# The first 512 tokens' attention output stored as two float16 halves and turned by transposing DMAs, and the sums of squares spread by one bfloat16 product

## The chip, the cores and the metric

The kernel runs on one core of one Trainium2 chip. Its engines are named here as the profile names them: PE (TensorE, matrix products), PEld (its loading of weights), DVE (VectorE), ACT (ScalarE), POOL (GpSimd) and SP (SyncE, which here does nothing but issue DMAs). Each engine runs its own instructions strictly in order, and an instruction that waits holds back all that stand behind it on that engine. The metric is the device time of one execution in microseconds (us), less being better.

## The reference

One decoder layer over 2048 tokens of width 1024, in which two mixers share a normalised input and one output projection:

```python
h = rms_norm(x, g_pre[l]) * (1.0 + scale[:, None, :]) + shift[:, None, :]
proj = h @ w_in[l]
qa, ka, va, fa, za, qb, kb, vb, zb = jnp.split(proj, split_points, axis=-1)
oa = forgetting_attention(qa, ka, va, fa + b_fgate[l])     # 8 heads of 64, causal
oa = oa * jax.nn.silu(za)
qb, kb = rope(qb, positions), rope(kb, positions)
ob = sliding_window_sink_attention(qb, kb, vb, sinks[l])   # window of 128, 8 query heads
ob = ob * jax.nn.silu(zb)
y = jnp.concatenate([oa, ob], axis=-1) @ w_out[l]
x = x + gate[:, None, :] * rms_norm(y, g_post[l])
```

(The reshapes into heads are left out.) What matters for the change is the piece between the two attentions and the last product: the attention output `o` of 2048 x 1024, with tokens as rows, is multiplied elementwise by the gates `z` and then enters the product with `w_out`. For that product the features must lie on the partitions, so `o` has to be turned (transposed) on its way.

## The kernel before

**Stages.** The 2048 tokens are 16 tiles of P = 128, or 4 chunks of CH = 512, numbered `ci`; the 1024 features are KT = 8 slices of 128. The stages follow one another: normalisation, the input projection with the window attention beside it, the forgetting attention of heads 0 to 7 (20 steps to a head, two key blocks of 128 to a step: two steps for chunk 0, then four, six and eight), and the output projection of tiles 0 to 15, whose first pieces are mixed into the steps of head 7. Large products are made of float16 halves: a float32 value is written as `hi + lo`, with `hi` its float16 rounding and `lo` the rest, and three float16 products take the place of one in float32.

**Order of the work.** The program is one hand-made list. A counter `tick()` advances twice in each attention step, and `after(n, f)` puts `f` into the list n ticks later. Each engine executes its instructions in the order in which that list issues them; waits come from data and from buffers in use.

**Attention step.** On PE the scores (L1349, L1350, on the diagonal L1352) write one buffer `sta`; ACT takes the exponential (L1356, `p`) and its float16 half (L1360, `pha`); DVE takes the rest by a subtraction (L1363); two steps later PE multiplies by the values (L1373, L1375, L1376). There is one `sta`, so the scores of the next step wait for L1356. At a chunk's last step DVE normalises the sum into `ona` (L1380, L1382).

**Storing the attention output.** `o_store` (L283) takes a result of 512 tokens (64 features of a head) to memory. For chunks 1 to 3 ACT makes the float16 half (L295, after `lag` ticks), one tick later DVE makes the rest (L291), and one DMA stores both (L292) into `o_d[ci]`, which holds the two halves of each tile. For chunk 0 one DMA stores the float32 values at once (L285). The window attention issues these DMAs on POOL, the forgetting attention on SP. The gates `z` are written to memory earlier, already turned (`z_d`).

**Turning it.** `Out.load` (L1464) brings one tile's `o` and gates into pieces of two buffers `T`, all of it issued by SP: for tiles 0 to 3 a plain load of the 128 x 1024 float32 rows (L1479), for tiles 4 to 15 two transposing DMAs (L1483), one for each half; then the gates (L1485). `Out.turn(lag)` (L1487) follows some ticks later. For tiles 0 to 3 it begins with eight PE transposes (L1492) into two PSUM banks `px`. Then, each in a tick of its own: `gate` on DVE, which for tiles 0 to 3 multiplies the two banks by the gates (L1502) and for the others first adds the halves (L1505) and then multiplies (L1506); `squares_` on ACT (L1510), which sums the squares along each partition into `gs`; `scale_`, where PE multiplies `gs` by a matrix of ones (L1514) so that each partition receives the total, and DVE makes a power of two of it (L128, L129, L1518, L1519); then the scaled halves for the product, on ACT (L1524) and on DVE (L1525). The product itself is L1576 on PE.

**When.** The loads of tiles 0 and 1 are issued at steps 4 and 6 of head 7, their turns at steps 6 and 8; those of tiles 2 and 3 come with the first pieces of the output projection, all inside head 7, which ends at about 1000 us. Around them SP also loads the output weights (L1433), which ACT and DVE split into halves `wohl` (L1442, L1443), and two rows of row maxima for the scores (L1263). L392 and L396 belong to the gates of the last heads, L351 to their projection.

Of the kernel before, what the change touches and what calls it, by code (L numbers as in the profile page):

```python
# [10 lines left out]
F32 = mybir.dt.float32  # L11
F16 = mybir.dt.float16
BF16 = mybir.dt.bfloat16
# [3 lines left out]
ALU = mybir.AluOpType  # L17
AX = mybir.AxisListType

P = 128  # L20
S = 2048
D = 1024
KT = D // P
NB = S // P
CH = 512
NCH = S // CH
# [17 lines left out]
def hybrid_layer(  # L44
# [17 lines left out]
    V, A, G, PE, SP = nc.vector, nc.scalar, nc.gpsimd, nc.tensor, nc.sync  # L62
# [6 lines left out]
    dram = ctx.enter_context(tc.tile_pool(name="dram", bufs=1, space=DRAM))  # L69
# [5 lines left out]
    const = ctx.enter_context(tc.tile_pool(name="const", bufs=1))  # L75
    small = ctx.enter_context(tc.tile_pool(name="small", bufs=4))

    o_d = [dram.tile([CH, D], F32, name="o_d0")] + [dram.tile([4, 2, P, D], F16, name=f"o_d{t}") for t in range(1, NCH)]
    z_d = dram.tile([KT, P, S], F32, name="z_d")
    mx_d = [dram.tile([P, 1], F32, name=f"mx_d{n}") for n in range(3)]  # L80

# [1 line left out]
    def sm(n, tag):  # L83
        return small.tile([P, n], F32, tag=tag, name=tag)
# [71 lines left out]
    ident = const.tile([P, P], F32, name="ident")  # L156
# [8 lines left out]
    ones = const.tile([P, P], F32, name="ones")  # L165
# [36 lines left out]
    def after(n, f):  # L202
        late.append([n, f])
# [77 lines left out]
        w_low(key, 0, 1)  # L281

    def o_store(on, pool, ci, rows_, cols_, eng, lag):  # L283
        if ci == 0:
            eng.dma_start(o_d[0][rows_, cols_].rearrange("(u p) c -> p u c", p=P), on)  # L285
            return
        u0, u1 = rows_.start // P, rows_.stop // P
        oh = pool.tile([P, u1 - u0, 2, on.shape[-1]], F16, tag="oh", name="oh")

        def low():  # L290
            V.tensor_tensor(oh[:, :, 1], on, oh[:, :, 0], op=ALU.subtract)  # L291
            eng.dma_start(o_d[ci][u0:u1, :, :, cols_].rearrange("u n p c -> p (u n) c"),  # L292
                          oh[:].rearrange("p u n c -> p (u n) c"))

        after(lag, lambda: A.activation(oh[:, :, 0], on, AF.Copy))  # L295
        after(lag + 1, low)
# [166 lines left out]
    start = ExitStack()  # L463
# [998 lines left out]
    class Out:  # L1462
# [5 lines left out]
        def load(self):  # L1468
            t = self.t
            rows_ = slice(t * P, (t + 1) * P)  # L1470
            n = t % 2 if t < 4 or t % 4 > 1 else 2 + t % 2
            T, n = Ts[n // 2], n % 2
            if T is Ts[0]:
                o, z = T[:, n, :], T[:, 2 + n, :]
            else:
                o, z = T[:, 2 * n, :], T[:, 2 * n + 1, :]
            if t < 4:
                self.o = o.bitcast(F32)
                SP.dma_start(self.o, o_d[0][rows_, :])  # L1479
            else:  # L1480
                self.oT = o.rearrange("p (l k n) -> p l k n", l=2, k=KT)
                for n in range(2):
                    SP.dma_start_transpose(self.oT[:, n], o_d[t // 4][t % 4, n])  # L1483
            self.z = z.bitcast(F32).rearrange("p (k n) -> p k n", k=KT)
            SP.dma_start(self.z, z_d[:, :, rows_].rearrange("k p n -> p k n"))  # L1485

        def turn(self, lag):  # L1487

            if self.t < 4:
                px = [bk[bank()][:].rearrange("p (k n) -> p k n", k=4) for _ in range(2)]  # L1490
                for k in range(KT):
                    PE.transpose(px[k // 4][:, k % 4, :], self.o[:, k * P:(k + 1) * P], ident[:])  # L1492
            self.hl = wpool.tile([P, 2, KT, P], F16, tag=("whl", "wraw")[self.t % 2], name="oz")
            self.sc = sm(1, "w_pw")
            hi, lo = self.hl[:, 0], self.hl[:, 1]
            gs = sm(1, "w_mx")

            def gate():
                if self.t < 4:
                    for h in range(2):  # L1500
                        z = self.z[:, 4 * h:4 * h + 4, :]
                        V.tensor_tensor(z, px[h], z, op=ALU.mult)  # L1502
                    return
                of = ozp.tile([P, KT, P], F32, tag="of", name="of")
                V.tensor_tensor(of[:], self.oT[:, 0], self.oT[:, 1], op=ALU.add)  # L1505
                V.tensor_tensor(self.z, of[:], self.z, op=ALU.mult)  # L1506

            def squares_():
                junk = stp.tile([P, KT, P], BF16, tag="st", name="zj")
                A.activation(junk[:], self.z, AF.Square, accum_out=gs[:])  # L1510

            def scale_():
                pg = bk[bank()][:, 0:1]
                PE.matmul(pg, ones[:], gs[:], start=True, stop=True)  # L1514
                root_scale(self.sc[:], pg)

                self.inv = sm(1, "w_sw")
                V.tensor_tensor(self.inv[:], self.sc[:], ysc[:], op=ALU.mult)  # L1518
                V.reciprocal(self.inv[:], self.inv[:])  # L1519

            after(1, gate)
            after(2, squares_)
            after(lag, scale_)
            after(lag + 1, lambda: A.activation(hi, self.z, AF.Copy, scale=self.sc[:]))  # L1524
            after(lag + 2, lambda: V.scalar_tensor_tensor(lo, self.z, self.sc[:], hi, op0=ALU.mult, op1=ALU.subtract))  # L1525
# [258 lines left out]
```

## Time and profile before

| | us |
|---|---|
| three executions | 1157.04, 1157.98, 1157.98 |
| their median | 1157.98 |
| the profiled execution | 1157.8 |
| its span, first to last instruction | 1156.1 |
| PE busy | 1116.8 (97%) |
| DVE busy | 930.5 (80%) |
| ACT busy | 661.4 (57%) |
| POOL busy | 207.5 (18%) |
| DMA, the whole span | 120.10 MB, mean 104 GB/s |

The profiled execution's time lies 1.7 us above its span: this is what passes around the first and the last instruction. A row of the time line gives the start in us, the duration in us, the engine (with q behind it: its sequencer, which issues and waits), the line of the kernel, the operation, `output<-input`, the shape, and in square brackets how long the engine stood idle just before and which engine, tile and line released it. `x8` in such a row means that eight instructions of a kind in a row are shown as one. Buffer numbers are left out, so `bk` is any PSUM bank and `T` any of the two big buffers. A row of the windows gives for a stretch of time the busy time of each engine with its number of instructions, the granted clock of PE, the busy share of the DMA engines, and what they moved.

### The profile page before, as it was taken

To read this page: it belongs to the slowest core of one execution; us is meant where nothing else is said; L and a number is where in the kernel's file an instruction comes from. 1 tells how busy PE (TensorE), PEld (TensorE's weight loads), DVE (VectorE), ACT (ScalarE), POOL (GpSimd) and SP (SyncE) were. 2 spreads that over 40 slices of the span, in tenths; PEclk is the share of its full clock that TensorE was granted. 3 is DMA by queue.
4 is the path that set the end of the run, shared out by engine and by line. 5 is a ranking of instruction groups with operands and counts; after the bars stand their busy time and mean duration, and the time that the engine had idled before them with its cause. 6 is when DMAs were issued, how large, how long until landed. Compare 5 with 4: busy or idle time off the path is not lost. (4 is left out here: it accounts for less than half of the span.)

```text
span 1156.1 us, 25291 instructions
## 1 busy us (share of the span) xinstructions
PE 1116.8 (97%) x9869; PEld 656.3 (57%) x9869; DVE 930.5 (80%) x2137; ACT 661.4 (57%) x1150; POOL 207.5 (18%) x332
## 2 busy tenths in 40 slices
PE   5899999999999999999999999999999999999997
PEld 2475544577765866555555555555555555544444
DVE  7877468987888568788988899888888887878885
ACT  2876344654555421666757666666776778534332
POOL 1122134554556530010010110001000000000000
PEclk9899999999999999999999999999999999999999
DMA  9943355433243232442344342123311337686743
GB/s 333 336 116 72 87 78 96 97 63 90 52 92 88 58 87 58 73 108 29 80 64 87 84 67 70 38 49 76 45 43 34 91 101 206 140 225 197 199 135 109
DMA packets 123476, 120.10 MB, mean 104 GB/s; under 512 B 64948, under 2 KB 100828, under 8 KB 123356
## 3 DMA queue, kind: packets, MB, share of 16 engines
q1 hardware_dynamic: 112088, 85.69, 27.6%
q0 software_dynamic: 10832, 32.50, 13.5%
q8 instruction: 77, 1.26, 0.6%
q14 instruction: 43, 0.35, 0.1%
q10 hardware_dynamic: 436, 0.28, 0.1%
HBM read 64.75 MB, written 25.18 MB: 78 GB/s over the span
## 5 line engine op out<-in xcount | busy, mean ns | idle before, releaser
L1356 ACT ACTIVATE p<-sta,lift,scl_qk 128x1024 f32<-128x1024 f32 (+2 forms) x160 | 172.0, 1075 | 131.6 <-PE sta L1350 82.6
L351 PE MATMUL bk<-hT,wh_qk 128*128 128x512 f16 x768 | 194.7, 378 | 0.0
L1363 DVE TENSOR_TENSOR pha<-p,pha 128x1024 f16<-128x1024 f32 (+2 forms) x160 | 169.1, 1057 | 0.2 <-ACT pha L1360 0.2
L1303 DVE TENSOR_REDUCE a_m<-bk 128x1 f32<-128x512 f32 x192 | 130.4, 686 | 45.8 <-PE bk L1300 44.8
L1576 PE MATMUL bk<-wohl,oz 128*128 128x512 f16 x744 | 165.3, 379 | 1.1 <-DVE oz L1525 0.7
L1360 ACT ACTIVATE pha<-p 128x1024 f16<-128x1024 f32 (+2 forms) x160 | 148.1, 926 | 5.9 <-PE poa L1376 1.2
L1576 PEld LDWEIGHTS <-oz 128*128 128x128 f16 x744 | 71.9, 99 | 82.8 <-DVE oz L1525 1.8
L1376 PE MATMUL poa<-vt,pha 128*128 128x65 f16 x1088 | 116.1, 192 | 1.4 <-DVE pha L1363 1.2
L1373 PE MATMUL poa<-vt,pha 128*128 128x65 f16 x1088 | 116.6, 193 | 0.8 <-DVE ona L1382 0.7
L1375 PE MATMUL poa<-vt,pha 128*128 128x64 f16 x1088 | 116.6, 194 | 0.0
L351 PEld LDWEIGHTS <-wh_qk 128*128 128x128 f16 x768 | 72.1, 97 | 74.4 <-issue 2.1
L1349 PE MATMUL sta<-T 128*128 128x512 f16 (+1 forms) x320 | 110.9, 346 | 2.8 <-ACT p L1356 2.7
L1300 PE MATMUL bk<-T 66*128 66x512 f16 (+2 forms) x320 | 109.7, 348 | 2.4 <-DVE a_m L1303 1.9
L1373 PEld LDWEIGHTS <-pha 128*128 128x128 f16 x1088 | 101.5, 96 | 15.5 <-DVE ona L1382 1.9
L1350 PE MATMUL sta<-T 69*128 69x512 f16 (+1 forms) x320 | 109.8, 348 | 0.0
L1375 PEld LDWEIGHTS <-pha 128*128 128x128 f16 x1088 | 100.9, 97 | 11.4
L1376 PEld LDWEIGHTS <-pha 128*128 128x128 f16 x1088 | 100.8, 99 | 1.8 <-DVE pha L1363 1.7
L351 PE MATMUL bk<-hT,wh_za 128*128 128x512 f16 x384 | 99.7, 378 | 0.0
L369 PE MATMUL bk<-wh_va,hT 128*128 128x256 f16 x768 | 91.9, 273 | 0.0
L351 PE MATMUL bk<-hT,wh_zb 128*128 128x512 f16 x384 | 91.6, 379 | 0.2 <-DVE qc L754 0.2
L351 PE MATMUL bk<-hT,wh_qb 128*128 128x512 f16 x384 | 91.2, 379 | 0.0
L369 PEld LDWEIGHTS <-hT 128*128 128x128 f16 x768 | 73.3, 98 | 12.2 <-issue 2.1
(459 smaller groups left out, 1919.7 us busy)
## 6 DMA issues: line engine op xcount, KB each, us to landing
hT<-in_x_dram SPq DMA_DIRECT2D x20, 512.0 KB
wa<-in_w_ada_dram SPq DMA_DIRECT2D x16, 512.0 KB
z_d<-tz POOLq DMA_DIRECT2D x32, 256.0 KB, 3.0
T<-z_d SPq DMA_DIRECT2D x16, 512.0 KB
T<-stq SPq DMA_DIRECT2D x62, 128.0 KB
out_dram<-hT SPq DMA_DIRECT2D x15, 512.0 KB
xt<-in_x_dram SPq DMA_DIRECT2D x12, 512.0 KB
qs<-qf SPq DMA_DIRECT2D x80, 64.0 KB
```

The lines of the kernel that those rows point to most:

```text
L351: PE.matmul(ps, whl[:, a, k, :], hT[ci][:, b, k, :], start=(k == 0 and n == 0), stop=(k == KT - 1 and n == 2))
L369: PE.matmul(ps[:, (u % 2) * 2 * P:(u % 2 + 1) * 2 * P], hT[ci][:, a, k, u * P:(u + 1) * P], wv[p][:, b, k, :], start=(k == 0 and n == 0), ...
L1303: V.tensor_reduce(m3[:, u, pc:pc + 1], mx[:, :w], axis=AX.X, op=ALU.max)
L1349: PE.matmul(self.st[:, o:o + w], T[:, 3, kb_], T[:, 1, qc], start=True, stop=False)
L1350: PE.matmul(self.st[:, o:o + w], T[0:XR, 2, kb_], T[0:XR, 0, qc], start=False, stop=not diag)
L1356: A.activation(self.p32[:, :self.w], self.st[:, :self.w], AF.Exp, scale=scl[f"qk{self.hd}"][:], bias=lift[:])
L1360: A.activation(self.ph[:, 0, :self.w], self.p32[:, :self.w], AF.Copy)
L1363: V.tensor_tensor(self.ph[:, 1, :self.w], self.p32[:, :self.w], self.ph[:, 0, :self.w], op=ALU.subtract)
L1373: PE.matmul(po[:, u, :], ph[:, 0, pq], vt[:, b, hd, 0:65], start=(self.first and n == 0 and u == 0), stop=False)
L1375: PE.matmul(po[:, u, 0:64], ph[:, 0, pq], vt[:, b, hd, 65:VW], start=False, stop=False)
L1376: PE.matmul(po[:, u, :], ph[:, 1, pq], vt[:, b, hd, 0:65], start=False, stop=(self.last and n == len(self.blocks) - 1))
L1576: PE.matmul(py, self.hl[:, i, k, :], w_slot(8 * j + k)[:, cc], start=(k == 0 and m_ == 0), stop=(k == KT - 1 and m_ == 2))
```

## The change

`o_d[0]` gets the form that the other chunks have, so the special case for chunk 0 in `o_store` is gone: the eight float32 stores of the window attention and the eight of the forgetting attention become a copy on ACT, a subtraction on DVE and a store of the two halves. Each of tiles 0 to 3 is loaded by two transposing DMAs in place of one plain load, and its eight PE transposes are gone. Its `gate` now adds the two halves into a PSUM bank and multiplies that bank by the gates, bank by bank, which is four DVE operations of 128 x 512 where there were two. For all 16 tiles the product that spreads `gs` over the partitions takes the upper 16 bits of its float32 operands as bfloat16, which drops the lower bits of the sums; the result sets only a power of two, by which a tile is scaled for its float16 halves and which is divided out again.

```diff
-    o_d = [dram.tile([CH, D], F32, name="o_d0")] + [dram.tile([4, 2, P, D], F16, name=f"o_d{t}") for t in range(1, NCH)]
+    o_d = [dram.tile([4, 2, P, D], F16, name=f"o_d{t}") for t in range(NCH)]
...
     def o_store(on, pool, ci, rows_, cols_, eng, lag):
-        if ci == 0:
-            eng.dma_start(o_d[0][rows_, cols_].rearrange("(u p) c -> p u c", p=P), on)
-            return
         u0, u1 = rows_.start // P, rows_.stop // P
...
-            if t < 4:
-                self.o = o.bitcast(F32)
-                SP.dma_start(self.o, o_d[0][rows_, :])
-            else:
-                self.oT = o.rearrange("p (l k n) -> p l k n", l=2, k=KT)
-                for n in range(2):
-                    SP.dma_start_transpose(self.oT[:, n], o_d[t // 4][t % 4, n])
+            self.oT = o.rearrange("p (l k n) -> p l k n", l=2, k=KT)
+            for n in range(2):
+                SP.dma_start_transpose(self.oT[:, n], o_d[t // 4][t % 4, n])
...
                 px = [bk[bank()][:].rearrange("p (k n) -> p k n", k=4) for _ in range(2)]
-                for k in range(KT):
-                    PE.transpose(px[k // 4][:, k % 4, :], self.o[:, k * P:(k + 1) * P], ident[:])
...
             gs = sm(1, "w_mx")
+            gs1 = gs[:].bitcast(BF16)[:, 1:2]
...
                     for h in range(2):
-                        z = self.z[:, 4 * h:4 * h + 4, :]
-                        V.tensor_tensor(z, px[h], z, op=ALU.mult)
+                        hs = slice(4 * h, 4 * h + 4)
+                        V.tensor_tensor(px[h], self.oT[:, 0, hs], self.oT[:, 1, hs], op=ALU.add)
+                        V.tensor_tensor(self.z[:, hs], px[h], self.z[:, hs], op=ALU.mult)
                     return
...
-                PE.matmul(pg, ones[:], gs[:], start=True, stop=True)
+                PE.matmul(pg, ones[:].bitcast(BF16).rearrange("p (n two) -> p two n", two=2)[:, 1], gs1, start=True, stop=True)
```

Lines behind `o_store` have numbers that are three smaller after the change, and those behind the removed transposes differ by more.

The order of the instructions shows two places. The first is SP in head 7, from the last stores of chunk 0 and 3 to the loads of tiles 0 and 1 (`o_d_69` is chunk 0's, `sv` and `hT_110` take output weights). Before:

```order
L292 DMA o_d_72<-oh 128x8x64
L1433 DMA sv<-in_w_out_dram 128x512
L285 DMA o_d_69<-ona 128x4x64
L1479 DMA T_6055<-o_d_69 128x1024
L1485 DMA T_6055<-z_d 128x8x128
L1263 DMA T_6056<-rw 2x4x128
L1433 DMA hT_110<-in_w_out_dram 128x512
L1479 DMA T_6055<-o_d_69 128x1024
L1485 DMA T_6055<-z_d 128x8x128
```

With the change:

```order
L289 DMA o_d_72<-oh 128x8x64
L1430 DMA sv<-in_w_out_dram 128x512
L289 DMA o_d_69<-oh 128x8x64
L1476 DMA_TRANSPOSE T_6079<-o_d_69 128x8x128 x2
L1478 DMA T_6079<-z_d 128x8x128
L1260 DMA T_6080<-rw 2x4x128
L1430 DMA hT_110<-in_w_out_dram 128x512
L1476 DMA_TRANSPOSE T_6079<-o_d_69 128x8x128 x2
L1478 DMA T_6079<-z_d 128x8x128
```

No DMA has changed its place; the store now takes its data from `oh`, which DVE writes two ticks after `ona`, and two transposing DMAs stand where the plain loads stood.

The second place is DVE in the same stretch, from the step behind chunk 0's last result to the gate of tile 0. Before:

```order
L1320 TENSOR_SCALAR lq_1696<-a_mr 128x4
L1363 TENSOR_TENSOR pha<-p_13661,pha 128x1024
L392 TENSOR_SCALAR tz<-tz,bk_6030 128x512
L1363 TENSOR_TENSOR pha<-p_13707,pha 128x896
L1443 TENSOR_SCALAR wohl<-sv,wsc,wohl 128x512
L1363 TENSOR_TENSOR pha<-p_13755,pha 128x384
L1443 TENSOR_SCALAR wohl<-sv,wsc,wohl 128x512
L1502 TENSOR_TENSOR T_6055<-bk_138,T_6055 128x512
L1502 TENSOR_TENSOR T_6055<-bk_136,T_6055 128x512
L1363 TENSOR_TENSOR pha<-p_13801,pha 128x1024
```

With the change:

```order
L1360 TENSOR_TENSOR pha<-p_13706,pha 128x1024
L288 TENSOR_TENSOR oh<-ona,oh 128x4x64
L389 TENSOR_SCALAR tz<-tz,bk_6054 128x512
L1360 TENSOR_TENSOR pha<-p_13752,pha 128x896
L1440 TENSOR_SCALAR wohl<-sv,wsc,wohl 128x512
L1360 TENSOR_TENSOR pha<-p_13804,pha 128x384
L1440 TENSOR_SCALAR wohl<-sv,wsc,wohl 128x512
L1494 TENSOR_TENSOR bk_138<-T_6079 128x512
L1495 TENSOR_TENSOR T_6079<-bk_138,T_6079 128x512
L1494 TENSOR_TENSOR bk_136<-T_6079 128x512
L1495 TENSOR_TENSOR T_6079<-bk_136,T_6079 128x512
L1360 TENSOR_TENSOR pha<-p_13850,pha 128x1024
```

The new subtraction (L288) on which the store waits stands behind a step's subtraction of 128 x 1024; the gate has its two additions (L1494) more, and the next step's subtraction stands behind all four.

## Prediction

> **What bounds the kernel now.** First I read the page's head and the busy shares, then the windows of the last three hundred microseconds.
>
> ```profile
> span 1156.1 us, 25291 instructions
> PE 1116.8 (97%) x9869; PEld 656.3 (57%) x9869; DVE 930.5 (80%) x2137; ACT 661.4 (57%) x1150; POOL 207.5 (18%) x332
> ...
> 800.00:900.00 100.00, 99.91 (x1022) 57.80 (x1020) 86.87 (x201) 69.13 (x85) 3.84 (x7) 1.00 0.22 43
> 900.00:1000.00 100.00, 94.76 (x1073) 57.69 (x1071) 82.58 (x160) 79.62 (x104) 1.62 (x3) 1.00 0.46 128
> 1000.00:1100.00 100.00, 99.86 (x480) 47.09 (x479) 81.08 (x200) 37.30 (x67) 0.00 (x0) 1.00 0.79 207
> ```
>
> PE sets the time. From 800 to 900 and from 1000 to 1100 it is busy for more than 99.8% at a granted clock of 1.00, so what other engines gain or lose there costs nothing until it makes PE wait. The one stretch with slack is 900 to 1000, head 7, where PE lacks 5.2 us and ACT is at its busiest (79.6). That is where tiles 0 to 3 are loaded and turned. So I read the time lines there, PE and ACT first.
>
> ```profile
> 952.46 1.04 PE L1492 MATMUL bk<-ident,T 128*128 128x128 f32 x8
> ...
> 956.72 0.38 PE L1349 MATMUL sta<-T 128*128 128x512 f16 x1 [0.66 <-ACT p L1356]
> ...
> 965.47 0.27 PE L1349 MATMUL sta<-T 128*128 128x256 f16 x1
> ...
> 981.80 1.04 PE L1492 MATMUL bk<-ident,T 128*128 128x128 f32 x8
> 982.75 0.38 PE L1349 MATMUL sta<-T 128*128 128x512 f16 x1
> ```
>
> ```profile
> 954.42 1.06 ACT L1510 ACTIVATE sv<-T 128x1024 bf16<-128x1024 f32 x1 [0.75 <-DVE T L1502]
> ...
> 955.48 1.19 ACT L1356 ACTIVATE p<-sta,lift,scl_qk 128x1024 f32<-128x1024 f32 x1
> ...
> 962.08 1.06 ACT L1510 ACTIVATE sv<-T 128x1024 bf16<-128x1024 f32 x1
> ...
> 963.14 1.08 ACT L1356 ACTIVATE p<-sta,lift,scl_qk 128x896 f32<-128x896 f32 x1
> ...
> 985.33 1.06 ACT L1510 ACTIVATE sv<-T 128x1024 bf16<-128x1024 f32 x1
> ...
> 1005.39 1.06 ACT L1510 ACTIVATE sv<-T 128x1024 bf16<-128x1024 f32 x1 [4.36 <-DVE T L1502]
> ```
>
> This is the chain on which everything below rests. ACT waits 0.75 us for tile 0's gate (released by DVE L1502), makes the squares (954.42), and only then the exponential of the next step (955.48), and PE then waits 0.66 us for that exponential before its scores (956.72). A gate that ends later therefore moves the squares, the exponential, the single score buffer and PE one for one: there is no slack left to take it up. For the gate itself DVE:
>
> ```profile
> 946.22 1.22 DVE L1363 TENSOR_TENSOR pha<-p,pha 128x1024 f16<-128x1024 f32 x1
> 947.35 0.68 DVE L392 SCALAR_TENSOR_TENSOR tz<-tz,bk 128x512 f32<-128x512 f32 x1
> ...
> 953.10 1.29 DVE L1502 TENSOR_TENSOR T<-bk,T 128x512 f32<-128x512 f32 x2 [2.03 <-PE bk L1492]
> ...
> 960.76 1.28 DVE L1502 TENSOR_TENSOR T<-bk,T 128x512 f32<-128x512 f32 x2
> ...
> 984.01 1.28 DVE L1502 TENSOR_TENSOR T<-bk,T 128x512 f32<-128x512 f32 x2
> ...
> 1004.07 1.29 DVE L1502 TENSOR_TENSOR T<-bk,T 128x512 f32<-128x512 f32 x2
> ...
> 1008.31 1.22 DVE L1505 TENSOR_TENSOR of<-T 128x1024 f32<-128x1024 f16 x1
> 1009.62 1.23 DVE L1506 TENSOR_TENSOR T<-of,T 128x1024 f32<-128x1024 f32 x1
> ```
>
> Gates end at 954.39, 962.04, 985.29 and 1005.36, and the squares start at 954.42, 962.08, 985.33 and 1005.39: in all four tiles at once.
>
> **The change part by part.** The sum is made against the profiled execution, 1157.8 us (span 1156.1 and 1.7 around it); the median of the runs, 1157.98, lies 0.2 above.
>
> *Tile 0's loads.* SP now, and how long two transposing DMAs hold it (a later tile's pair, the nearest that the time line shows whole):
>
> ```profile
> 944.86 0.38 SPq L285 DMA_DIRECT2D o_d<-ona  x1
> 946.91 0.33 SPq L1479 DMA_DIRECT2D T<-o_d  x1
> 947.47 0.37 SPq L1485 DMA_DIRECT2D T<-z_d  x1
> ...
> 948.70 0.34 SPq L1433 DMA_DIRECT2D hT<-in_w_out_dram  x1
> ...
> 1033.99 2.86 SPq L1483 DMA_TRANSPOSE T<-o_d  x2
> 1036.96 0.52 SPq L1485 DMA_DIRECT2D T<-z_d  x1
> ```
>
> ```profile
> L1502 DVEq EVENT_SEMAPHORE  x4: 21/21/21, 952.3 to 1004.0; - x4
> L291 DVE TENSOR_TENSOR oh<-ona,oh x24: 414/418/426, 493.4 to 1001.7; 128x256 f16<-128x256 f32 x24
> L295 ACT ACTIVATE oh<-ona x24: 399/400/417, 490.6 to 1000.6; 128x256 f16<-128x256 f32 x24
> ```
>
> Today the store goes out at 944.86, as soon as the values are normalised. With the change the halves come first. The order puts the new subtraction behind the step's L1363 (946.22), in the place of L392, so it starts at 947.35 and takes 0.42 (L291): the store goes out at 947.8, 2.9 later. The load behind it waits for the store to land; it started 2.05 after the store (944.86 to 946.91), and the new store moves the same 128 KB, so the transposes start at 949.8. Two of them keep SP for 2.97 until the gates' load (1033.99 to 1036.96); the plain load took 0.56 (946.91 to 947.47). So the gates' load leaves at 952.8 and not at 947.47, 5.3 later.
>
> When it lands no row says directly. It is the same load as now, and the one issued at 947.47 had landed when DVE's sequencer was past its wait at 952.3: at most 4.8 us. From below, the store's 2.05 is the shortest round trip shown, and this load has 384 KB more, which at the highest rate of the page's second part,
>
> ```profile
> GB/s 333 336 116 72 87 78 96 97 63 90 52 92 88 58 87 58 73 108 29 80 64 87 84 67 70 38 49 76 45 43 34 91 101 206 140 225 197 199 135 109
> ```
>
> 336 GB/s, take 1.2: at least 3.2. The gates of tile 0 are there between 956.0 and 957.6. The first addition needs only the two halves and is done by then; what follows is a multiplication, an addition and a multiplication. Two multiplications of 128 x 512 took 1.29 in a row, 0.60 for the first and 0.68 for the second; and where an operation reads what the one before it wrote, the next began 1.31 after a start (1008.31 to 1009.62) though it was busy for 1.22, so 0.09 more. That is 0.60 + 0.77 + 0.68 = 2.05, and the gate ends between 958.1 and 959.7 instead of 954.39: 3.7 to 5.3 later. I take **5.2**, near the upper end, because the upper row is the same load. By the chain above all of it reaches PE. The eight transposes taken from PE at 952.46 give nothing back, since they stood ahead of that wait. What is queued behind the gate on DVE is the next step's L1363, and PE's products with the values wait for that; they are late together with it, not in addition.
>
> The trace's row for the transposes is 2.86 us for two on SP, against 0.33 for a plain load. [...]
>
> *The gates of tiles 1 to 3.* Tile 1's turn stands two steps behind its loads, as tile 0's does, and what follows tile 0 is late together with it, so I price no second wait for loads, only the longer gate: 0.77 + 0.60 + 0.77 + 0.68 = 2.82 instead of 1.29, 1.5 more, at a place where the squares follow the gate at once. Each can cost 0 to 1.5. For **tile 1** PE has some margin: the exponential behind the squares (963.14 + 1.08) ends at 964.2 and the scores start at 965.47, 1.3 later; but ACT has further work behind it in that step, and I take 1.0. For **tile 2** PE loses eight transposes (981.80 to 982.75, 0.95 of PE), but the scores behind them wait for ACT's exponentials sooner or later, and ACT is the late one: 1.4. For **tile 3** PE already waits for the squares, by the weight load of L1514:
>
> ```profile
> 1006.59 0.30 PEld L1514 LDWEIGHTS bk<-w_mx,ones 128*128 128x128 f32 x2 [0.48 <-ACT sv L1510]
> ```
>
> so 1.5. Together 3.9, with bounds of 0 and 4.5, and less still if the removed transposes of tiles 2 and 3 (0.95 each) shorten PE's way.
>
> *The product over the partitions.*
>
> ```profile
> 1055.61 0.28 PE L1514 MATMUL bk<-w_mx,ones 128*128 128x1 f32 x2
> 1055.75 1.02 PE L1576 MATMUL bk<-wohl,oz 128*128 128x512 f16 x4
> ...
> 939.82 0.19 PE L1373 MATMUL poa<-vt,pha 128*128 128x65 f16 x1
> 939.86 0.19 PE L1375 MATMUL poa<-vt,pha 128*128 128x64 f16 x1
> ```
>
> It holds PE for 0.14 (1055.61 to 1055.75). A single 16-bit product of 64 columns holds it for 0.04 (939.82 to 939.86), and one column can't be longer. So 0.10 for each tile that PE doesn't wait for anyway, 14 of 16: **−1.4** (bounds: 0, and −2.2 for all of 16 times 0.14).
>
> *The sixteen new copies and subtractions.* 0.40 us of ACT (L295) and 0.42 of DVE (L291) each, eight beside the window attention and eight in the heads. Where PE is busy for 99.9% (800 to 900) DVE has 13 us and ACT 31 us to spare in 100, and chunks 1 to 3 have 24 of the same pairs in the heads already. Hidden under PE; if the cover were gone, at one of ACT's or DVE's turns each, 16 times 0.4 or 6.4. I take **+0.3**. The output weights that stand behind tile 0's loads on SP (948.70) leave some 5 us later and are used from 960 on, when everything else is later too: nothing.
>
> The sum is 5.2 + 1.0 + 1.4 + 1.5 − 1.4 + 0.3 = **+8.0**, that is 1165.8 by the profiled execution, and with 0.2 for the median **1166.0 us**.
>
> **The rivals.** *Faster: the loads are in time.* If SP gave out the transposes as quickly as plain loads (2.4 earlier) and the subtraction ran ahead of L1363 (1.1 earlier), the gates' load would leave at 949.2 and land, by the lower bound of 3.2, at 952.4. The point from which it decides is 952.3: from there 2.05 more still ends at today's 954.39. Then only savings are left, 1.9 of PE's transposes in tiles 2 and 3 and 1.4 of products, against 0.3: 1157.98 − 3.0 = 1155.0. Against it speak the 2.86 us of SP and the order on DVE; it needs both. *Only tile 0 pays.* The longer gates of tiles 1 to 3 disappear in slack (PE's 1.3 at tile 1 is for it, the back-to-back squares against it) and PE keeps the two tiles' transposes: 5.2 − 1.9 − 1.4 + 0.3 = +2.2, 1160.2. [...]
>
> ```profile
> L1483 SPq DMA_TRANSPOSE T<-o_d x24: 1244/1480/3466, 981.3 to 1098.6; - x24
> ```
>
> *Slow transposes.* The slowest issue there took 3.47 us; two of them hold SP for 6.9, 4.0 more than 2.97: 1170.0. For it speaks that head 7 is where weights are loaded beside them, against it the median of 1.48. *The new product is no shorter* (its weights are then waited for): the sum without the −1.4, 1167.4, is inside the forecast's own spread.
>
> **How the numbers follow.** The forecast has 0.57, the slow transposes 0.15, only tile 0 pays 0.13, the quick issue 0.10, the loads in time 0.05. From its terms' bounds the forecast alone spans 1163 to 1168.5; the range reaches down to the second rival and up past the fourth, 1160.0 to 1170.5, and leaves out the first and the tails of the others, some 0.12. What a measurement can tell from no change is about 0.2%, 2.3 us, so slower begins at 1160.3: faster 0.05 (the first rival, 0.25% below), same 0.07 (half of the second, which lies on the bound), slower 0.88.
>
> **What would show it.** In the new time line: tile 0's store out at about 947.8, its gates' load at 952.8, its gate's last multiplication ending near 959.6, squares and exponential right behind, and PE idle for some 5 to 6 us before the scores in place of 0.66; four DVE operations of together 2.8 in each of the four gates; the product at one pass; no new idle time of PE before 940. It is wrong if PE's idle time before those scores is below 3 us, if the loss lies ahead of head 7, or if the time comes out below 1160.

## The result, and the profile after

The change made the kernel slower: 1167.76 us (median of four executions, 1165.92 to 1170.40) against 1157.98 us before, in the same session, a ratio of 1.0087 with a 95% interval of 1.0065 to 1.0110 (taken over all executions; the two medians alone give 1.0084). The forecast was 1166.0 with a range of 1160.0 to 1170.5. The profiled execution of the change took 1166.6 us, 8.8 more than that of before.

The head and the busy shares of the page of the change, then the windows that were shown of before:

```profile
span 1164.9 us, 25251 instructions
PE 1117.2 (96%) x9821; PEld 651.9 (56%) x9821; DVE 942.8 (81%) x2161; ACT 668.1 (57%) x1166; POOL 207.4 (18%) x332
```

```profile
800.00:900.00 100.00, 99.91 (x1044) 58.20 (x1042) 86.42 (x201) 69.81 (x88) 3.85 (x7) 1.00 0.21 41
900.00:1000.00 100.00, 87.11 (x928) 50.28 (x926) 81.70 (x152) 75.47 (x98) 1.63 (x3) 0.97 0.52 120
1000.00:1100.00 100.00, 96.84 (x545) 45.41 (x542) 81.30 (x199) 39.02 (x69) 0.00 (x0) 1.00 0.76 197
```

PE is busy for as long as before (1117.2 us) although it has 48 products fewer (9821 against 9869); some of those left ran at a granted clock of 0.50, as shown below. Up to 940 it is busy for 913.0 us, where it was 911.0, so no new idle time lies there. The loss stands between 940 and 1020: PE lacks 12.9 us in the second window where it lacked 5.2, and 3.2 in the third where it lacked 0.1. The time line of SP in the change, at the loads of tiles 0 and 1:

```profile
949.04 0.40 SPq L289 DMA_DIRECT2D o_d<-oh  x1
951.42 2.73 SPq L1476 DMA_TRANSPOSE T<-o_d  x2
954.37 0.80 SPq L1478 DMA_DIRECT2D T<-z_d  x1
...
956.48 3.32 SPq L1476 DMA_TRANSPOSE T<-o_d  x2
```

Its VectorE, from the normalisation of chunk 0 to the gates of tiles 0 to 3:

```profile
945.66 0.42 DVE L1379 TENSOR_TENSOR ona<-poa,a_ri 128x256 f32<-128x256 f32 x1
...
948.60 0.42 DVE L288 TENSOR_TENSOR oh<-ona,oh 128x256 f16<-128x256 f32 x1
...
957.25 0.70 DVE L1494 TENSOR_TENSOR bk<-T 128x512 f32<-128x512 f16 x1 [4.84 <-DMA T<-o_d]
959.19 0.69 DVE L1495 TENSOR_TENSOR T<-bk,T 128x512 f32<-128x512 f32 x1 [1.24 <-DMA T<-z_d]
...
960.52 0.69 DVE L1495 TENSOR_TENSOR T<-bk,T 128x512 f32<-128x512 f32 x1
...
969.65 0.69 DVE L1495 TENSOR_TENSOR T<-bk,T 128x512 f32<-128x512 f32 x1
...
994.34 0.69 DVE L1495 TENSOR_TENSOR T<-bk,T 128x512 f32<-128x512 f32 x1
...
1015.32 0.69 DVE L1495 TENSOR_TENSOR T<-bk,T 128x512 f32<-128x512 f32 x1
```

And who waits for it, on ACT and on PE:

```profile
961.25 1.06 ACT L1503 ACTIVATE sv<-T 128x1024 bf16<-128x1024 f32 x1 [6.33 <-DVE T L1495]
...
970.38 1.06 ACT L1503 ACTIVATE sv<-T 128x1024 bf16<-128x1024 f32 x1 [1.36 <-DVE T L1495]
```

```profile
962.45 0.16 PE L1507 MATMUL bk<-w_mx,ones 128*128 128x1 bf16 x1 [6.14 <-ACT sv L1503]
963.54 0.58 PE L1346 MATMUL sta<-T 128*128 128x512 f16 x1 [0.93 <-ACT p L1353]
```

The reader sees the chain of the prediction with its waits: the halves late (4.84), the gates z after them (1.24), then squares, sums and exponential one behind the other, and PE idle for 6.14 us. That idle time stands ahead of the product for the sums, which waits for the squares, and only 0.93 more ahead of the scores, where the prediction had put all of it. Before the change PE came to the same product without a wait. Its row, and that of chunk 0's normalisation, before:

```profile
955.78 0.28 PE L1514 MATMUL bk<-w_mx,ones 128*128 128x1 f32 x2
...
944.41 0.42 DVE L1382 TENSOR_TENSOR ona<-poa,a_ri 128x256 f32<-128x256 f32 x1
```

z was issued at 954.37, but its data did not move until the halves were through. The trace has the data in packets, 2048 of 256 bytes for the halves and 1024 of 512 bytes for z. What moved in the change from 952.8 to 956.4, and from 956.5 to 958.6:

```profile
DMA packets 2016, 0.52 MB, mean 146 GB/s; under 512 B 2015, under 2 KB 2015, under 8 KB 2015
DMA packets 1082, 0.63 MB, mean 298 GB/s; under 512 B 26, under 2 KB 1028, under 8 KB 1082
```

z's first packet started at 956.45, 2.1 us after its issue; a plain load with nothing ahead of it started 1.0 after its own (949.76 to 950.73 in e8). The prediction has z held back by SP's issue; in the trace the landing of the halves ahead of it holds it back as well.

To compare executions that did not start alike, I count from the start of chunk 0's normalisation (L1379 in the change, L1382 before) to the end of tile 0's gate, from gate to gate, and from tile 3's gate to the end of the span:

| kernel (profiled execution) | ratio to before, 95% interval | to gate 0 | to gate 1 | to gate 2 | to gate 3 | to the end |
|---|---|---|---|---|---|---|
| before | 1 | 9.98 | 7.65 | 23.25 | 20.07 | 150.74 |
| the change | 1.0087, 1.0065 to 1.0110 | 15.55 | 9.13 | 24.69 | 20.98 | 148.89 |
| e1, product only | 0.9981, 0.9972 to 0.9990 | 9.98 | 7.65 | 23.20 | 19.97 | 149.17 |
| e2, float32 product | 1.0093, 1.0079 to 1.0107 | 16.06 | 9.13 | 24.66 | 20.96 | 150.43 |
| e3, z just ahead | 1.0082, 1.0069 to 1.0096 | 15.86 | 9.13 | 24.66 | 20.96 | 148.85 |
| e4, subtraction early | 1.0078, 1.0064 to 1.0092 | 15.35 | 9.12 | 24.67 | 20.97 | 148.88 |
| e5, z early | 1.0076, 1.0061 to 1.0091 | 14.36 | 9.13 | 24.66 | 20.97 | 148.86 |
| e6, turn later | 1.0093, 1.0077 to 1.0110 | 15.75 | 6.06 | 31.27 | 18.67 | 148.92 |
| e7, PE kept busy | 1.0089, 1.0074 to 1.0104 | 15.86 | 9.13 | 25.15 | 20.96 | 148.89 |
| e8, plain halves | 1.0074, 1.0059 to 1.0089 | 14.95 | 9.12 | 24.67 | 20.96 | 148.88 |
| e9, plain and z early | 1.0059, 1.0044 to 1.0074 | 13.38 | 9.13 | 24.66 | 20.96 | 150.20 |
| e10, no additions | 1.0033, 1.0020 to 1.0045 | 15.52 | 7.67 | 23.59 | 19.94 | 148.86 |
| e11, z and subtraction early | 1.0064, 1.0048 to 1.0080 | 13.73 | 9.12 | 24.66 | 20.97 | 148.83 |
| e12, e9 and subtraction early | 1.0056, 1.0041 to 1.0071 | 11.74 | 9.13 | 24.66 | 20.95 | 148.89 |

The intervals between gates repeat to 0.03 us wherever nothing touches them, so the columns tell parts of the change apart that the whole times, which scatter over 1 to 5 us, do not. The way to gate 0 repeats less well: the change, e2 and e7 have the same work up to there and took 15.55, 16.06 and 15.86. A difference of less than about 0.5 us in that column shows nothing.

### The profile page after: what moved, and what is told of

Read it like the earlier page. It is cut to its first block, busy times and chain, and to the rows that moved or that the text cites. A ratio compares the mean times of both kernels' runs of the same rounds, so it can differ in the third digit from the quotient of the medians.

```text
span 1164.9 us, 25251 instructions
## 1 busy us (share of the span) xinstructions
PE 1117.2 (96%) x9821; PEld 651.9 (56%) x9821; DVE 942.8 (81%) x2161; ACT 668.1 (57%) x1166; POOL 207.4 (18%) x332
```

## The experiments

**e1_product_only**, the kernel before with the new product alone:

```diff
-                PE.matmul(pg, ones[:], gs[:], start=True, stop=True)
+                PE.matmul(pg, ones[:].bitcast(BF16).rearrange("p (n two) -> p two n", two=2)[:, 1], gs1, start=True, stop=True)
```

> The kernel before with only the bfloat16 product for the sums of squares. My theory: each product holds TensorE 0.11 us less (the output tiles follow each other 10.49 us apart in the trace of before and 10.38 in that of the change), on 14 to 16 tiles: 1.4 to 1.8 us faster than before, about 1156.4. Rival: the pitch of the tiles has another cause and the product saves nothing: 1158.0. It is also a control for the 1.25 us that the change has lost ahead of head 7: with this kernel's first instructions being those of before, the first L1363 subtraction should start near 467.4 as before if the stores of chunk 0 cost that loss; if executions scatter there by themselves, it may be anywhere up to 468.7.

1154.73 us against 1157.41, ratio 0.9981 (0.9972 to 0.9990): faster, and the only kernel here that beats both. Its stores of output tile 2 and, twelve tiles later, of the last ones, on SP (a row that takes three DMAs together starts with the first):

```profile
1021.19 0.34 SPq L1607 DMA_DIRECT2D out_dram<-hT  x1
...
1141.81 8.20 SPq L1607 DMA_DIRECT2D out_dram<-hT  x3
```

They are 120.62 us apart where those of before,

```profile
1023.12 0.34 SPq L1606 DMA_DIRECT2D out_dram<-hT  x1
...
1144.99 8.20 SPq L1606 DMA_DIRECT2D out_dram<-hT  x3
```

are 121.87, so 0.104 of each tile; the whole way from normalisation to end is 1.72 shorter (211.69 to 209.97), as my theory had it. The control in it did not settle what it was for: head 0 began at 465.95, earlier than before (467.44), though nothing ahead of it differs.

**e2_fp32_product**, the change without the new product (the diff of e1 reversed).

> The change with the float32 product put back: stores in halves and transposing DMAs alone. My theory: 1.4 to 1.8 us slower than the change, so 1168.2 where a profiled execution of the change took 1166.6, and tiles 10.49 us apart again. Rival: no difference to the change.

1167.95 us. The last column of the table is 1.54 longer than in the change, and the tiles follow as before, so the product is worth the same in both kernels. The whole times (1.0093 and 1.0087) can't tell them apart. This execution carries all 16 new copies and subtractions, and its first subtraction of head 0 started at 467.56, 0.12 after that of before.

**e3_gates_first**, in `load`, for tiles 0 to 3:

```diff
+            if t < 4:
+                SP.dma_start(self.z, z_d[:, :, rows_].rearrange("k p n -> p k n"))
             for n in range(2):
                 SP.dma_start_transpose(self.oT[:, n], o_d[t // 4][t % 4, n])
-            SP.dma_start(self.z, z_d[:, :, rows_].rearrange("k p n -> p k n"))
+            if t >= 4:
+                SP.dma_start(self.z, z_d[:, :, rows_].rearrange("k p n -> p k n"))
```

> The change, with the gates z of tiles 0 to 3 loaded ahead of the two transposing DMAs and not behind them. My theory: SP's 2.9 us of transposes no longer hold z back; the gate of tile 0 then starts when the second half has landed (957.25 in the trace of the change) and takes 2.75 in a row, so it ends at 960.0 and not at 961.2: 1.2 us faster than the change, about 1165.4, no more, because the halves themselves bind next. Rival 1: z still sets the end since it shares the DMA engines: no difference. Rival 2: z in front delays the transposes by its own 0.8 of issue and its data: 1 us slower than the change.

My theory fell: gate 0 ends 15.86 after the normalisation (15.55 in the change; 14.4 was expected). SP and VectorE of this kernel:

```profile
948.96 0.39 SPq L1477 DMA_DIRECT2D T<-z_d  x1
950.80 3.70 SPq L1479 DMA_TRANSPOSE T<-o_d  x2
```

```profile
958.04 0.70 DVE L1497 TENSOR_TENSOR bk<-T 128x512 f32<-128x512 f16 x1 [6.36 <-DMA T<-o_d]
```

No wait for z is left, but the halves are used 7.24 us after their issue (950.80 to 958.04), where it was 5.83 (951.42 to 957.25). What z no longer waits for, the halves now do: z's packets move until 953.3, and those of the halves from 952.9 on. SP's issue of two transposes took 3.70 in place of 2.73 beside it.

**e4_early_sub**, in `o_store`:

```diff
-        after(lag + 1, low)
+        after(lag + (ci > 0 or lag > 1 or eng is not SP), low)
```

> The change, with head 7's subtraction for chunk 0 issued ahead of the step's L1360 on VectorE and not behind it. My theory: the subtraction starts at 947.46 and not at 948.60, the store, the transposes, the gates' load and tile 0's gate all move up by 1.1 us, and so does the end: about 1165.5 against 1166.6. Rival: another wait (the DMA engines, busy with output weights) sets the landing, and the time does not move.

```profile
946.41 0.42 DVE L1379 TENSOR_TENSOR ona<-poa,a_ri 128x256 f32<-128x256 f32 x1
...
957.96 0.70 DVE L1494 TENSOR_TENSOR bk<-T 128x512 f32<-128x512 f16 x1 [4.80 <-DMA T<-o_d]
```

```profile
948.67 0.39 SPq L289 DMA_DIRECT2D o_d<-oh  x1
...
951.03 2.77 SPq L1476 DMA_TRANSPOSE T<-o_d  x2
```

The store left 2.26 after the normalisation and not 3.38, and the transposes 4.62 and not 5.76, as meant. But the halves were used 11.55 after it, as in the change (11.59), and gate 0 gained 0.2, less than that column's scatter. So the rival's outcome held: a transfer that leaves 1.1 earlier does not land earlier here. Its cause stays open. Counted from the normalisation, the packets of the halves start at 6.21 and end at 10.76, where the change has 7.20 and 10.83, so they start 1.0 earlier and take as much longer. POOL's store of gates, which one would suspect, is through at 6.30 (952.71) and so moves beside them for no more than 0.1 us.

**e5_gates_early**: `load` split in two, z of tiles 0 and 1 at steps 2 and 3.

```diff
+            if hd == 7 and r in (2, 3):
+                outs[r - 2].load("z")
             if hd == 7 and r in (4, 6):
-                outs[r // 2 - 2].load()
+                outs[r // 2 - 2].load("o")
```

> The change, with the gates z of tiles 0 and 1 loaded at steps 2 and 3 of head 7, ahead of chunk 0's store, so that behind the store only the transposing DMAs stand. My theory after the first runs: the transposes themselves hold the DMA engines (5.8 us from issue to use for 512 KB, while the engines were over 100% busy at some 75 to 200 GB/s), and z behind them adds a tail of 1.2 us of waiting and one product. Without it tile 0's gate starts when the halves are there and takes 2.75 in a row: 1.2 to 1.9 us faster than the change, ratio to before about 1.007. Rival: the issue on SticE alone sets the pace (SP's 2.9 us), so taking z from behind it brings 2.9 or more. Rival 2: no gain, as when z was put directly ahead of the transposes, because the transposes land later whatever shares the engines with them.

(The engine meant in its first rival is SP.)

```profile
953.93 2.71 SPq L1477 DMA_TRANSPOSE T<-o_d  x2
```

```profile
959.72 0.70 DVE L1497 TENSOR_TENSOR bk<-T 128x512 f32<-128x512 f16 x1 [4.84 <-DMA T<-o_d]
...
961.79 0.69 DVE L1498 TENSOR_TENSOR T<-bk,T 128x512 f32<-128x512 f32 x1
```

Gate 0 gains 1.19 (14.36) against the change, and up to 1.70 against e2, which is what my theory said: it now runs in a row (2.76), and starts when the halves are there, 5.79 after their issue as in the change.

**e6_later_turn**, in the main loop:

```diff
-            if hd == 7 and r < 8:
-                npn = N_LAST + (len(punits) - N_LAST) * (r + 1) // 8 - pos[0]
-            if hd == 7 and r >= 8:
-                npn, fil = N_IN * (r - 8) // (NS - 9) - opos[0], ofill
+            if hd == 7 and r < 9:
+                npn = N_LAST + (len(punits) - N_LAST) * (r + 1) // 9 - pos[0]
+            if hd == 7 and r >= 9:
+                npn, fil = N_IN * (r - 9) // (NS - 10) - opos[0], ofill
...
-            if hd == 7 and r in (6, 8):
-                outs[r // 2 - 3].turn(3)
+            if hd == 7 and r in (7, 8):
+                outs[r - 7].turn(3)
```

> The change, with tile 0's turn one step of head 7 later (step 7), tile 1's left at step 8, the last gate projections spread over nine steps and not eight, and the output products begun a step later. My theory: tile 0's 6.3 us of idle time of ScalarE is a wait for landing data; one step more of other work (2.9 to 4.1 us between exponentials there) covers as much of it, so the kernel is 3 to 4 us faster than the change: 1163 or so, ratio to before 1.005 to 1.006. Rival: the tiles' own chain (gate, squares, scale, halves, products) is what takes longer, and moving it shifts the loss without shrinking it: no difference, or slower because the products are squeezed into fewer steps.

1168.32 us; the rival held. The landing is where it was (gate 0 at 15.75), one more step of attention lies ahead of it, and gate 1 comes 2.9 earlier than in the change (15.75 + 6.06 against 15.55 + 9.13). But the output products then crowd: gate 2 is 3.7 later, and the windows show PE starved first and full behind.

```profile
960.00:970.00 10.00, 4.38 (x34) 2.40 (x33) 8.58 (x17) 7.95 (x11) 0.00 (x0) 0.60 1.16 245
970.00:980.00 10.00, 8.92 (x77) 5.31 (x78) 6.68 (x11) 5.70 (x8) 0.54 (x1) 0.72 0.94 201
980.00:990.00 10.00, 10.00 (x94) 5.38 (x93) 6.21 (x9) 8.52 (x12) 0.00 (x0) 1.00 0.38 98
```

Work that PE can't do while it waits has to be done later, and from 980 on it has no room for it.

**e7_busy_tensor**, in `scale_` of tile 0:

```diff
+                b_ = bank()
+                for _ in range(26 if self.t == 0 else 0):
+                    PE.matmul(bk[b_][:].rearrange("p (u c) -> p u c", u=4), identh[:], vt[:, 0:4, 0, 0:P], start=True, stop=True)
-                pg = bk[bank()][:, 0:1]
+                pg = bk[b_][:, 0:1]
```

> The change, with 26 products of 128x512 that nobody uses ahead of tile 0's product for the sums, so that TensorE is busy while it waits for the landing data. It tests whether the lower granted clock after the wait (0.58 and 0.74 between 960 and 970 in the trace of the change) is part of the loss. My theory: the clock stays near 1.00, and the time is the same within 0.5 us, since from tile 0's squares to tile 1's gate ScalarE and VectorE work without a gap (3.97 us from squares to the scaled halves, as before the change) and TensorE is not the one waited for. Rival: the slow clock costs 1.5 us or more (4.84 busy us at 0.74), and the kernel is that much faster than the change, with less scatter between executions.

Two windows of the change, then the same of this kernel (the third number from the right is the granted clock):

```profile
961.00:963.00 2.00, 0.16 (x1) 0.10 (x1) 1.93 (x6) 1.75 (x3) 0.00 (x0) 0.50 0.91 249
963.00:965.00 2.00, 1.46 (x4) 0.55 (x4) 1.93 (x6) 2.00 (x4) 0.00 (x0) 0.50 0.55 183
```

```profile
961.00:963.00 2.00, 2.00 (x11) 0.88 (x9) 1.97 (x4) 0.19 (x1) 0.00 (x0) 1.00 1.21 213
963.00:965.00 2.00, 0.34 (x2) 0.10 (x1) 1.86 (x7) 2.00 (x4) 0.00 (x0) 1.00 0.85 210
...
967.00:969.00 2.00, 1.03 (x2) 0.13 (x2) 1.21 (x2) 2.00 (x3) 0.54 (x1) 0.50 0.62 139
```

The products kept the clock at 1.00 where the change has 0.50, but it was halved all the same at 966.6, behind two idle times of 0.83 and 0.93 us, so half of what I expected of the clock failed. The time was the same (1168.16, ratio 1.0089), and gate 1 came 9.13 after gate 0 as in the change. That alone does not clear the clock, since between the two gates it was halved in both kernels, for 6.4 us in the change and for 5.3 here. A later run does: e10 had the clock at 0.50 from 959.0 to 969.3, nearly all the way from gate 0 (961.84) to gate 1 (969.51), and took the 7.67 us that the kernel before takes at full clock. The slow clock is thus no part of tile 1's loss. Gate 2 came 0.5 later here (25.15), with the clock low until 973.4; how much it costs where PE does set the pace this run can't say.

**e8_plain_halves**, for tiles 0 to 3 in `load`:

```diff
-                SP.dma_start_transpose(self.oT[:, n], o_d[t // 4][t % 4, n])
+                if t < 4:
+                    SP.dma_start(self.oT[:, n], o_d[0][t, n].rearrange("p (k n) -> p k n", k=KT))
+                else:
+                    SP.dma_start_transpose(self.oT[:, n], o_d[t // 4][t % 4, n])
```

> The change, with two plain DMAs of the same 256 KB each in place of the transposing ones for tiles 0 to 3; the halves of these tiles arrive unturned, so the first 512 tokens of the output are not the reference's. Everything else, and each wait, stays. My theory: transposing costs tile 0 twice, 2.1 us in SP's issue (0.4 a load and not 1.4) and, since the engines are held at a low rate, 1 to 2 us more in the landing: 3 to 4.5 us faster than the change, ratio to before 1.005. Rival: the transposes are as fast as plain DMAs once issued: 2.1 us and no more. Rival 2: the longer chain alone (copy, subtraction, store, wait) is the loss: less than 1 us.

```profile
949.76 0.80 SPq L1477 DMA_DIRECT2D T<-o_d  x2
950.79 0.37 SPq L1481 DMA_DIRECT2D T<-z_d  x1
```

```profile
953.86 0.70 DVE L1497 TENSOR_TENSOR bk<-T 128x512 f32<-128x512 f16 x1 [3.08 <-DMA T<-o_d]
956.94 0.69 DVE L1498 TENSOR_TENSOR T<-bk,T 128x512 f32<-128x512 f32 x1 [2.38 <-DMA T<-z_d]
```

Both halves of my theory show in the rows, and neither in the time. SP is through in 1.03 and not 2.95 (the change: 951.42 to 954.37), and 512 KB are used 4.10 after issue and not 5.83. But z, issued 1.9 earlier, now takes 6.15 to its use (950.79 to 956.94) where it took 4.82 (954.37 to 959.19), as the output weights and tile 1's loads follow as much sooner and share the engines: their packets move beside z's from 954.2 on. Gate 0 gains 0.6 against the change, hardly more than the scatter. Rival 2 held in its number; that the longer chain alone is the loss did not, as the combined kernels below show.

**e9_plain_early, e10_no_adds, e11_early_all, e12_plain_early_all.** The first is e8 and e5 together, the third e5 and e4, the fourth all three. The edit of e10, in `gate`:

```diff
-                        V.tensor_tensor(px[h], self.oT[:, 0, hs], self.oT[:, 1, hs], op=ALU.add)
-                        V.tensor_tensor(self.z[:, hs], px[h], self.z[:, hs], op=ALU.mult)
+                        V.tensor_tensor(self.z[:, hs], self.oT[:, 0, hs], self.z[:, hs], op=ALU.mult)
```

> Plain DMAs for the halves of tiles 0 to 3 (these 512 tokens arrive unturned and are not the reference's) and the gates z of tiles 0 and 1 loaded ahead of chunk 0's store: the two edits that brought 0.6 and 1.2 us alone, together. My theory: halves and gates are two paths of nearly the same length to the same multiplication, so one edit alone uncovers the other path; together the gate can start when the plain halves land (4.1 us after issue, where the transposed ones took 5.8) and ends 2.75 later. Counted from chunk 0's normalisation (the last DVE L1379 ahead of the gate), the gate of tile 0 then ends 12.6 us later where the change took 15.55 and before 9.98: 3.0 us faster than the change, more than the 1.8 that the two add up to. Rival: the edits add up, 1.8 us. Rival 2: the engines stay as busy as ever and it is 1.2 again.

> The change with z of tiles 0 and 1 loaded early and with head 7's subtraction for chunk 0 ahead of the step's L1360: the two cures that leave the result as it is. My theory: z no longer binds, so the 1.1 us by which the transposes leave earlier should now count, and the gate of tile 0 ends 1.2 + 1.1 earlier than in the change, counted from the normalisation 13.25 and not 15.55; 2.3 us faster than the change and still some 6 us slower than before. Rival: the transposes land at the same time however early they leave, as with the early subtraction alone (11.55 us after the normalisation, 11.59 in the change), because they share the engines with a store of POOL that starts with them: 1.2 only.

> Plain halves, z early and the subtraction early, all together (the first 512 tokens arrive unturned again). My theory: each link of the chain is then taken out but the store and its wait, so the gate of tile 0 ends 1.1 earlier than with plain halves and early z, 11.5 us after the normalisation (9.98 before), and 4.1 us earlier than in the change. Rival: another path, for instance the copy on ScalarE and the store's landing, keeps it at 12.6.

Gate 0 gained 2.17, 1.82 and 3.81 against the change (13.38, 13.73, 11.74). In e9 the halves took 4.86 after issue, not 4.10, and its gain lies between the theory (3.0) and the sum of its parts (1.8); from the sum it can't be told apart. In e11 the early subtraction was worth 0.63 beside early z, where alone it was worth 0.20, a difference within the scatter; in e12 it was worth 1.64 (13.38 to 11.74), more than its 1.1, since the halves landed faster too (4.33). So the links do not add: the three edits alone bring 2.0 in sum and together 3.81, where my theory said 4.1. The whole times follow roughly.

> The change without the four additions of halves in the gates of tiles 0 to 3: the gate multiplies the high halves alone, so the low halves of the first 512 tokens' attention output are left out. My theory: the longer gate stands in a chain of ScalarE and VectorE work without gaps, so from tile 0's gate to tile 1's it is 7.65 us again as before the change (9.13 in the change), to tile 2's 23.25 again (24.69), to tile 3's about 20.1 (20.98), and tile 0's own gate ends 0.7 earlier: 4 to 4.5 us faster than the change, ratio to before 1.005. Rival: these tiles lose their time to late loads or to the lower granted clock, the intervals stay as in the change, and only 0.7 is gained.

```profile
960.55 1.29 DVE L1494 TENSOR_TENSOR T<-T 128x512 f32<-128x512 f16 x2 [7.47 <-DMA T<-z_d]
968.22 1.29 DVE L1494 TENSOR_TENSOR T<-T 128x512 f32<-128x512 f16 x2
991.81 1.29 DVE L1494 TENSOR_TENSOR T<-T 128x512 f32<-128x512 f16 x2
1011.75 1.29 DVE L1494 TENSOR_TENSOR T<-T 128x512 f32<-128x512 f16 x2
```

The intervals went back to 7.67, 23.59 and 19.94, 3.6 us in sum, at a ratio of 1.0033; my theory held for tiles 1 to 3. For tile 0 it can't be told: z came 0.7 later than in the change and the shorter gate gained 0.03, but z is as late in e2 (14.04 after the normalisation, 13.53 in the change, 14.23 here), so this is that column's scatter. The whole time came down by more than these intervals explain (1162.05 against 1167.76); the rest I can't place.

## Why the prediction was right

By the table, the change against before from the normalisation on, beside the terms of the prediction:

| term | predicted | measured |
|---|---|---|
| tile 0, to gate 0 | +5.2 | +5.57 |
| tile 1 | +1.0 | +1.48 |
| tile 2 | +1.4 | +1.44 |
| tile 3 | +1.5 | +0.91 |
| products (last column) | −1.4 | −1.85 |
| 16 copies and subtractions | +0.3 | nothing in the heads; ahead of them not resolved |

From the normalisation to the end that is 7.55 against 7.7. The sum is nearer than its terms, four of which are off by 0.4 to 0.6 and cancel; that much is luck. And the span of 1163 to 1168.5 that the prediction gives for its forecast does not come out of the bounds that it lists, which with 0.3 for the copies reach from 1159.8 to 1168.1. **Tile 0** went link by link. The subtraction sits where the order showed it; the store left 2.93 later than before, counted from the normalisation (2.9 predicted), and the gates' load 2.95 behind the start of the transposes (2.97). z was used 4.82 after its issue, at the upper end of the range (3.2 to 4.8), and the gate ended 2.02 after that (2.05). Of the missing 0.4 the store's landing makes 0.33, 2.38 in place of 2.05. That it reaches PE is in the rows of ACT and PE above.

What the prediction had less well is the weight of the single links. It counted a quick issue of the transposes, two in the 0.56 that the plain load took, as 2.4 earlier, and gave it a chance of 0.10; no run shows transposes issued so: tile 0's two held SP for 2.71 (e5) to 3.70 (e3). Two plain loads in their place held it for 0.80 in e8, and that gave 0.6. The step that fails there is to take all other links as they were: z's landing and the halves' landing are two paths that end within 2 us of each other (used at 959.19 and 957.25 in the change). z's packets started only when the halves were through (956.45), and a transfer that was issued earlier did not land as much earlier: in e4 the transposes left 1.14 earlier and the halves were used 0.04 earlier, and in e8 z took 6.15 to its use and not 4.82, with the packets of what comes next beside its own from 954.2 on.

**Tiles 1 to 3** lose by the longer gate: e10 takes out the additions and the intervals return to within 0.35 us, and its tile 1 does so at a clock of 0.50. Why tile 3 loses 0.91 and not the 1.5 by which its gate is longer, no run shows. **The 32 removed transposes** were priced at nothing for tiles 0 to 3, and that held: with the additions gone, e10's intervals are 7.67, 23.59 and 19.94 against 7.65, 23.20 and 19.97 in e1, which still has all 32. PE's time was saved where PE then waits: for tile 0 its idle time grew by 6.4 us (6.14 and 0.93 against 0.66) while the gate came 5.57 later. **The product** was priced well for one tile (0.10, and 0.104 in e1) and a little low in sum: 1.72 in e1 from the normalisation to the end.

**Ahead of head 7** the change stood 1.25 behind before, where 0.3 was forecast. From the first subtraction of head 0 to the normalisation in head 7 both kernels took 476.97 us, so the seven copies and subtractions of heads 0 to 6 cost nothing, as the prediction said. What is left lies ahead of head 0, where the other eight stand, and stays open: the profiled executions start head 0 at 467.44 (before) and 465.95 (e1) without the new work, and between 467.05 (e8) and 471.05 (e5) in the twelve kernels with it, 468.9 on average. That looks like more than 0.3, perhaps 2 us, but with two executions on one side, 1.5 apart, it is not shown. The medians point the same way: they differ by 9.8, of which 7.55 lie behind the normalisation.

## What to carry to other kernels

Work taken off the busiest engine was worth nothing here where that engine waited for another (the intervals between gates in e10, without the 32 transposes, lie within 0.4 us of those in e1, which has them); look first at what stands in the bracket of its next instruction there. Data that is produced, stored, loaded turned and used within a few steps is a chain of landings, and a copy and a subtraction ahead of the store lengthened it (the store left 2.93 later); where two transfers feed one operation, curing one of them uncovered the other (plain halves alone gave 0.60, early z alone 1.19, both 2.17), so look at when the packets move and not only at when a load is issued. And a change of several parts is best taken apart: here the smallest, one product in place of two passes, was the only gain (0.104 us a tile), and alone it beats both kernels.

## What the runs showed of the hardware that was not expected

PE idled from 956.3 to 962.4 in the change; the granted clock fell to 0.50 at 960.8 and stayed there until 967.6, and a product of 128x512 took 0.58 (963.54) and not 0.38. Ahead of tile 3's sums a shorter wait did it in one kernel only: both in the change and in e9 PE idles for 2.34 us there, the change with its clock at 1.00, e9 with

```profile
1012.00:1014.00 2.00, 0.00 (x0) 0.00 (x0) 1.97 (x3) 0.86 (x1) 0.00 (x0) 1.00 1.02 167
1014.00:1016.00 2.00, 1.66 (x6) 0.66 (x6) 1.65 (x7) 0.32 (x3) 0.00 (x0) 0.66 0.69 156
1016.00:1018.00 2.00, 2.00 (x6) 0.67 (x5) 1.91 (x2) 1.78 (x3) 0.00 (x0) 0.50 0.95 299
```

and there PE does set the pace: e9's way from gate 3 to the end was 150.20, 1.3 longer than in its neighbours. How often the other executions of the change were hit so, the times alone don't show. In these two traces the clock changes only at whole multiples of 3.41 us from one another (960.77 and 967.60 in the change; 966.86, 1014.64 and 1018.05 in e9). Counted on in such steps, which is an estimate from these times, e9's gap of 2.34 us (1012.00 to 1014.34) falls whole into one step, 1011.23 to 1014.64; in the change a step ends at 1015.38, in the middle of the gap (1014.91 to 1017.24). That fits, but no run moved the gap to test it, and why a gap of 2.34 us can suffice no run here shows.

Two transposing DMAs of 256 KB took 5.83 us from issue to use (5.79 to 6.34 in e2, e5, e6 and e7) and two plain ones 4.10 (e8; 4.86 in e9, 4.33 in e12), some 1.5 more, and held SP 1.9 longer.
